# Branch B's scan: state products of two chunks in one visit, halves before full width, and the state update at once

## The chip, the core and the metric

One core of a Trainium2 chip runs one launch of a two-layer decoder trunk. The metric is the device time in microseconds (us) of that launch. TensorE (PE in the profile) does the matrix products, with weight loads shown apart as PEld; VectorE is DVE, ScalarE is ACT, GpSimd is POOL, and SP is the queue that issues nearly all DMA transfers.

## The reference, cut to what matters

Each layer normalises `x`, applies one wide input projection, and feeds four token mixers. Their outputs, each multiplied by a SiLU gate, are projected, merged by sigmoid gates, projected again and added to `x`. Mixer B is a gated DeltaNet with 4 heads and 256 tokens in 4 chunks of 64. Its scan over the chunks is what the change touches:

```python
def step(state, xs):
    q_i, k_i, u_i, w_i, qk_i, g_i = xs
    v_new = u_i - jnp.einsum('bhcd,bhde->bhce', w_i, state)
    o = (jnp.einsum('bhcd,bhde->bhce', q_i * jnp.exp(g_i)[..., None], state)
         + jnp.einsum('bhcm,bhme->bhce', qk_i, v_new))
    g_last = g_i[..., -1]
    state = (state * jnp.exp(g_last)[..., None, None]
             + jnp.einsum('bhcd,bhce->bhde', k_i * jnp.exp(g_last[..., None] - g_i)[..., None], v_new))
    return state, o
_, o = lax.scan(step, state0, xs)
```

The outputs `o` of all chunks are then RMS-normalised per head and go on to the gate.

## The kernel before, in words

All large weights are streamed from memory in pieces of 512 KB (`wr`, four buffers), cast on ACT to a high part (`wh`, L484) and split on DVE to a low part (`wl`, L485). A projection then runs three TensorE products for each piece: L594 to L596 for 512 columns (tiles `m`, `d`, `br`), L631 to L633 for 256 (tiles `z`, `b`). These follow each other as a list of items. The mixers are Python generators ("streams") that are advanced a step between two items: each `yield` ends a step, and what a step issues stands in program order there. The build then schedules the instructions of each engine by its own timeline, so a step's instructions come out interleaved with those of the items around it. On the chip each engine runs its list strictly in the order that results.

`branch_b` is such a stream. Its scan loops over `c` in 0..3. Two heads share a tile of 128 partitions (64 tokens each), so with `p` in 0, 1 a chunk is two such pairs. For each chunk:

- `pv` (L1075, L1078), the new values: for each `p` one product of full width (`U`, `vb`, out 128 partitions x 128 columns), then, where `c > 0`, two halves (`wT` with the state `st`), each of which writes 64 partitions. DVE copies `pv` to `vn` (L1081). Then the transposes `pot` of the chunk before (`out_T`, L1064).
- `po` (L1088, L1091), the outputs, after a `yield`: again, for each `p`, one product of full width (`Q`, `vn`), then two halves (`qgT`, `st`). ACT squares it (`sqo`), DVE sums (`ro`), DVE and POOL make the reciprocal root (`rsbo`, `ro`), DVE scales `po` to `on` (L1099).
- `pS` (L1107), the state's update, after another `yield`: four products with 64 rows each, two into each of two PSUM banks, and DVE adds them to the decayed state (`S`, L1114; L1111 for the first chunk).

So a chunk takes three visits. All of `pv`, `po`, `pS` and `pot` use the pool of two PSUM banks called "b"; tiles in SBUF come from a pool of 20 slabs "b", which the reloaded residual `xr` and the norm's weights `lng`, `lnb` share.

Three shapes of TensorE product matter: full (128 rows, 128 output partitions), halves (128 rows, 64 output partitions; the profile prints 128*64) and products of 64 rows (64*128; `pS`, and the scores `dsc` of mixer D). `dpo` of mixer D is also made of halves, and `dpt` of transposes of full width. An fp32 product of this size is two matmul records in the profile, a transpose one.

Of the kernel before, what the change touches and what calls it, by code (L numbers as in the profile page):

```python
# [15 lines left out]
ALU = mybir.AluOpType  # L16
# [4 lines left out]
P = 128  # L21
# [180 lines left out]
def kernel(ctx: ExitStack, tc: tile.TileContext, d, out, dbg=None, nlayers=DEPTH):  # L202
    nc = tc.nc
    V, A, T, G = nc.vector, nc.scalar, nc.tensor, nc.gpsimd
# [16 lines left out]
    def slab(which, shape, name):  # L221
        free = int(np.prod(shape[1:]))
        assert free <= 512, (name, shape)
        t = slabs[which].tile([P, 512], F32, tag="slab", name=name)[:shape[0], 0:free]
        if len(shape) == 3:
            t = t.rearrange("p (a b) -> p a b", b=shape[2])
        elif len(shape) == 4:
            t = t.rearrange("p (a b c) -> p a b c", b=shape[2], c=shape[3])
        return t

    def bank(which, shape, name):
        return banks[which].tile(shape, F32, tag=which, name=name)

    def fl(a):
        return a.rearrange("p a b -> p (a b)")
# [14 lines left out]
    def smc(name, i=0, n=1):  # L250
        lo = SM[name][0]
        return sm[:, lo + i:lo + i + n]
# [19 lines left out]
    def rstd(dst, src, bias, n, tag, mark=None):  # L272
        bt = tiny.tile([P, n], F32, tag=f"rsb{tag}", name=f"rsb{tag}")
        a = V.tensor_scalar(bt, src, bias, None, ALU.add)
        b = G.tensor_tensor(dst, bt, negh[:, 0:n], ALU.pow)
        if mark:
            marks[f"eps{mark}"], marks[f"pow{mark}"] = a, b
# [426 lines left out]
    def layer_items(l, prev):  # L704
# [161 lines left out]
        def branch_b():  # L866

            psel = bank("b", [P, 4, 2, 2, 2], f"psel{l}")
            for c in range(4):
                T.matmul(psel[:, c].rearrange("p k q h -> p (k q h)"), cfc("sel", c % 2), L.ckv[:, c // 2, 160:168],  # L870
                         start=True, stop=True)
            bd = sp.tile([P, 2, 4, 2], F32, tag="bd", name=f"bd{l}")
            for h2 in range(2):
                r = slice(64 * h2, 64 * h2 + 64)
# [28 lines left out]
            egl = sp.tile([P, 2, 8], F32, tag="b_egl", name=f"egl{l}")  # L903
# [9 lines left out]
            grp = []  # L913
            for g in range(2):
# [33 lines left out]
                vb = sb4("vb")  # L948
# [6 lines left out]
                kbg, ktil, qg = sb4("kbg"), sb4("ktil"), sb4("qg")  # L955
# [7 lines left out]
                qgT, dec = sb4("qgT"), sb4("dec")  # L963
                feat4([qgT], qg, "qg")
                pd = bank("b", [P, 4, P], f"pd{g}_{l}")
                for j in range(4):
                    T.matmul(pd[:, j, :], gcol[:, 4 * g + j:4 * g + j + 1].to_broadcast([P, P]), cfc("tri"),
                             start=True, stop=False)
# [4 lines left out]
                N, Q = sb4("N"), sb4("Q")  # L973
# [21 lines left out]
            for g in range(2):  # L995
                for j in range(4):
                    r = slice(32 * g + 8 * j, 32 * g + 8 * j + 8)
# [13 lines left out]
            for w in range(2):  # L1011
                for g in range(2):
                    for j in range(4):
                        r = slice(32 * g + 8 * j, 32 * g + 8 * j + 8)
                        nc.sync.dma_start(blocks(scr[1 + w, g], j), tb[r, w])
            yield
            inv = []
            for g in range(2):
                Ti, U = (slab("b", [P, 4, P], f"g_{nm}{g}_{l}") for nm in ("T", "U"))
                nc.sync.dma_start(fl(Ti), scr[1, g])  # L1020
                nc.sync.dma_start(fl(U), scr[2, g])
                inv.append((LLs[g], U, Ti))
            yield
            yield
            mk = lambda i: cu[:, i, :].unsqueeze(1).to_broadcast([P, 4, P])
            for li in range(2):
                Xs = []
                for g, (LL, U, Ti) in enumerate(inv):
                    px = bank("b", [P, 4, P], f"px{li}{g}_{l}")
                    for j in range(4):  # L1030
                        T.matmul(px[:, j, :], LL[:, j, :], U[:, j, :], start=True, stop=True)
                    Xs.append(slab("b", [P, 4, P], f"X{li}{g}_{l}"))
                    A.copy(Xs[g], px)
                yield
                for g, (LL, U, Ti) in enumerate(inv):
                    py = bank("b", [P, 4, P], f"py{li}{g}_{l}")
# [11 lines left out]
            wT = []  # L1048
# [10 lines left out]
            st = on = None  # L1059

            def out_T(c, on):
                pt = bank("b", [P, 2, 2, 64], f"pot{c}_{l}")
                for p in range(2):
                    T.transpose(pt[:, p].rearrange("p h i -> p (h i)"), on[:, p, :], ident)  # L1064
                for p in range(2):
                    A.activation(L.oT[1][p][:, :, 64 * c:64 * c + 64], pt[:, p], AF.Copy, scale=smc("onorm", l))

            for c in range(4):
                g = c // 2
                vb, ktil, qgT, _, Q, _ = grp[g]  # L1070
                U = inv[g][1]
                pv = bank("b", [P, 2, P], f"pv{c}_{l}")
                for p in range(2):
                    j = 2 * (c % 2) + p
                    T.matmul(pv[:, p, :], U[:, j, :], vb[:, j, :], start=True, stop=(c == 0))  # L1075
                    if c > 0:
                        for h2 in range(2):
                            T.matmul(pv[64 * h2:64 * h2 + 64, p, :], wT[g][:, j, 64 * h2:64 * h2 + 64],  # L1078
                                     st[:, 2 * p + h2, :], start=False, stop=True)
                vn = slab("b", [P, 2, P], f"vn{c}_{l}")  # L1080
                V.tensor_copy(vn, pv)  # L1081
                if on is not None:
                    out_T(c - 1, on)
                yield
                po = bank("b", [P, 2, P], f"po{c}_{l}")
                for p in range(2):
                    j = 2 * (c % 2) + p
                    T.matmul(po[:, p, :], Q[:, j, :], vn[:, p, :], start=True, stop=(c == 0))  # L1088
                    if c > 0:
                        for h2 in range(2):  # L1090
                            T.matmul(po[64 * h2:64 * h2 + 64, p, :], qgT[:, j, 64 * h2:64 * h2 + 64],  # L1091
                                     st[:, 2 * p + h2, :], start=False, stop=True)
                sq = slab("b", [P, 2, P], f"sqo{c}_{l}")
                A.activation(sq, po, AF.Square, scale=128.0 ** -0.5)
                ro = tiny.tile([P, 2], F32, tag="ro", name=f"ro{c}_{l}")
                V.tensor_reduce(ro, sq, AX.X, ALU.add)
                rstd(ro, ro, EPS, 2, "o")
                on = slab("b", [P, 2, P], f"on{c}_{l}")
                V.tensor_tensor(on, po, ro.unsqueeze(2).to_broadcast([P, 2, P]), ALU.mult)  # L1099
                if c < 3:  # L1100
                    yield
                    pS = [bank("b", [P, 2, P], f"pS{c}{h2}_{l}") for h2 in range(2)]
                    for p in range(2):
                        j = 2 * (c % 2) + p
                        for h2 in range(2):
                            r = slice(64 * h2, 64 * h2 + 64)
                            T.matmul(pS[h2][:, p, :], ktil[r, j, :], vn[r, p, :], start=True, stop=True)  # L1107
                    sn = slab("b", [P, 4, P], f"S{c}_{l}")
                    if c == 0:
                        for h2 in range(2):  # L1110
                            V.tensor_copy(sn.rearrange("p (q h) e -> p h q e", h=2)[:, h2], pS[h2])  # L1111
                    else:
                        for h in range(4):
                            V.scalar_tensor_tensor(sn[:, h, :], st[:, h, :],  # L1114
                                                   egl[:, h % 2, 2 * c + h // 2:2 * c + h // 2 + 1],
                                                   pS[h % 2][:, h // 2, :], ALU.mult, ALU.add)
                    st = sn
                yield
            out_T(3, on)


# [442 lines left out]
```

## Time and profile before

| what | value |
|---|---|
| median of 3 runs | 1056.73 us (1055.52 to 1058.17) |
| the profiled execution | 1053.03 us |
| its span, first to last instruction | 1050.9 us |
| PE busy | 1026.6 us, 98% |
| DVE, ACT, POOL busy | 718.8, 542.3, 27.3 us |
| mean granted TensorE clock | 0.993 of full speed |
| the scan in layer 0 | 288 to 374 us |
| the scan in layer 1 | 798 to 880 us |

The span is that of one profiled execution. Matmuls are pipelined and their ends are modelled, so what TensorE's work costs is read from the starts of its records: the time from one start to the next.

### The profile page before, as it was taken

What the parts mean: (1) busy time and instruction counts of PE and PEld (TensorE: products, weight loads), DVE (VectorE), ACT (ScalarE), POOL (GpSimd) and SP (SyncE); (2) the same over time, 40 slices, a digit from 0 to 9 for tenths busy, and PEclk for the clock granted to TensorE, in tenths of its full rate; (3) what the DMA queues carried; (4) which work ended last, traced back from release to release, by engine and by line L of the source; (5) the groups of instructions that cost most, each with busy time, mean ns of one, the idle gap of its engine ahead of it and who ended that gap; (6) DMA issues with size and microseconds to landing.
All of it is one profiled execution on the core that took longest, in us unless ns stands there. A gap on an engine that the chain in (4) does not pass through costs nothing.

```text
span 1050.9 us, 16072 instructions
## 1 busy us (share of the span) xinstructions
PE 1026.6 (98%) x5918; PEld 849.6 (81%) x5918; DVE 718.8 (68%) x1579; ACT 542.3 (52%) x1012; POOL 27.3 (3%) x37
## 2 busy tenths in 40 slices
PE   6999999999999999999999999999999999999996
PEld 6589897888887788888866998888789778888885
DVE  3788768886666656766684887798837555566676
ACT  2276675654453445555426567566545444555550
POOL 0000000000000000000000000000100000000000
PEclk9999999999999999999999999999999999999998
DMA  9973335557654476545824444456563337544551
GB/s 335 329 250 121 121 124 168 202 175 236 228 162 165 138 276 224 159 143 179 303 74 163 139 123 123 149 201 199 174 236 128 102 119 227 172 163 141 169 172 41
DMA packets 67406, 185.18 MB, mean 176 GB/s; under 512 B 13696, under 2 KB 17152, under 8 KB 67328
## 3 DMA queue, kind: packets, MB, share of 16 engines
q1 hardware_dynamic: 67328, 184.16, 52.7%
q8 instruction: 47, 0.77, 0.3%
q14 instruction: 31, 0.25, 0.1%
HBM read 179.67 MB, written 4.46 MB: 175 GB/s over the span
## 4 chain that ended last, share of the span: by engine, by line
PE 88%; DVE 4%; DMA 4%; ACT 1%; issue 1%; SPq 1%; DVEq 0%; ACTq 0%
PE m L594 6%; PE m L595 5%; PE m L596 5%; PE first L602 5%; PE d L594 4%; PE d L595 4%; PE d L596 4%; PE z L631 3%; PE z L632 3%; PE z L633 3%; PE br L594 3%; PE br L596 3%; PE br L595 3%; PE b L631 2%; PE b L632 2%; PE b L633 2%
## 5 line engine op out<-in xcount | busy, mean ns | idle before, releaser
L485 DVE TENSOR_TENSOR wl<-wr,wh 128x1024 fp32r<-128x1024 f32 x248 | 302.4, 1223 | 171.4 <-ACT wh L484 168.6
L484 ACT CAST wh<-wr 128x1024 fp32r<-128x1024 f32 x248 | 259.9, 1050 | 216.7 <-issue 41.9
L594 PE MATMUL m<-wh,hh 128*128 128x512 f32 x256 | 102.8, 401 | 0.4 <-DVE ml L1421 0.3
L594 PE MATMUL d<-wh,hh 128*128 128x512 f32 x256 | 103.0, 402 | 0.0
L595 PE MATMUL m<-wl,hh 128*128 128x512 f32 x256 | 101.9, 398 | 0.0
L595 PE MATMUL d<-wl,hh 128*128 128x512 f32 x256 | 101.2, 395 | 0.0
L596 PE MATMUL d<-wh,hl 128*128 128x512 f32 x256 | 101.1, 395 | 0.0
L596 PE MATMUL m<-wh,hl 128*128 128x512 f32 x256 | 100.6, 393 | 0.0
L631 PE MATMUL z<-hh,wh 128*128 128x256 f32 x256 | 74.1, 289 | 0.0
L632 PE MATMUL z<-hl,wh 128*128 128x256 f32 x256 | 73.4, 287 | 0.0
L633 PE MATMUL z<-hh,wl 128*128 128x256 f32 x256 | 73.3, 286 | 0.0
L305 DVE SCALAR_TENSOR_TENSOR ada<-wada,cact,ada 128x512 f32<-128x512 f32 x77 | 57.5, 747 | 18.7 <-DMA wada<-in_wada 17.9
L631 PE MATMUL b<-hh,wh 128*128 128x256 f32 x192 | 57.6, 300 | 2.8 <-ACT ckv L832 2.3
L594 PEld LDWEIGHTS m<-wh,hh 128*128 128x128 f32 x256 | 48.1, 188 | 11.8 <-issue 1.0
L596 PEld LDWEIGHTS d<-wh,hl 128*128 128x128 f32 x256 | 48.5, 189 | 10.4 <-issue 0.4
L595 PEld LDWEIGHTS d<-wl,hh 128*128 128x128 f32 x256 | 48.5, 190 | 9.8 <-DVE wl L485 0.3
L594 PEld LDWEIGHTS d<-wh,hh 128*128 128x128 f32 x256 | 48.5, 189 | 9.8 <-issue 0.6
L596 PEld LDWEIGHTS m<-wh,hl 128*128 128x128 f32 x256 | 48.1, 188 | 10.0 <-issue 0.3
L595 PEld LDWEIGHTS m<-wl,hh 128*128 128x128 f32 x256 | 48.1, 188 | 9.9 <-issue 1.0
L633 PE MATMUL b<-hh,wl 128*128 128x256 f32 x192 | 55.4, 288 | 0.0
L632 PE MATMUL b<-hl,wh 128*128 128x256 f32 x192 | 55.3, 288 | 0.0
L594 PE MATMUL br<-wh,bh 128*128 128x512 f32 x128 | 51.7, 407 | 0.0
(355 smaller groups left out, 2123.7 us busy)
## 6 DMA issues: line engine op xcount, KB each, us to landing
wr<-in_win SPq DMA_DIRECT2D x208, 512.0 KB
wr<-in_wbr SPq DMA_DIRECT2D x32, 512.0 KB
wada<-in_wada SPq DMA_DIRECT2D x32, 512.0 KB
wada<-in_wada SPq DMA_DIRECT2D x32, 256.0 KB
wro<-in_wout SPq DMA_DIRECT2D x8, 512.0 KB
wr<-in_wout SPq DMA_DIRECT2D x8, 512.0 KB
wrs<-in_win SPq DMA_DIRECT2D x8, 256.0 KB
wrearly<-in_win SPq DMA_DIRECT2D x8, 256.0 KB
```

The source lines that it names most:

```text
L305: return V.scalar_tensor_tensor(acc, w, cd, acc, ALU.mult, ALU.add)
L484: marks["hi"] = A.copy(hi, src)
L485: return [V.tensor_tensor(lo, src, hi.bitcast(F32), ALU.subtract)]
L594: ins.append(T.matmul(ps, a, wh, start=(first and i == 0), stop=False))
L595: ins.append(T.matmul(ps, a, wl, start=False, stop=False))
L596: ins.append(T.matmul(ps, b, wh, start=False, stop=(last and i == 1)))
L602: return [T.matmul(ps, a(2 * p + i, t), w[p](i * n, n), start=(first and i == 0), stop=(last and i == 1)) for i in range(2)]
L631: T.matmul(ps[:, f, :], wh, hh(k), start=(k == 0), stop=False)
L632: T.matmul(ps[:, f, :], wh, hl(k), start=False, stop=False)
L633: T.matmul(ps[:, f, :], wl, hh(k), start=False, stop=(k == nk - 1))
```

## The change

The scan is written with helpers: `from_state` issues the four halves of a chunk, `within` the two products of full width. The visit of chunk `c` now issues first the halves of `pv` for `c`, then (from `c = 2` on) the halves of `po` for `c - 1` with the state before (`before`), then the full products of `pv` for `c` and of `po` for `c - 1`. The accumulation's start flag moves with it, to the first product issued in a bank. The state's update `pS` follows in the next step, without the step that `po` had between. `out_T` is issued a step later than `normed`. The last chunk's outputs form a visit of their own. There are 8 steps where there were 11. No product, copy or transfer is added or taken away.

```diff
-            for c in range(4):
-                g = c // 2
-                vb, ktil, qgT, _, Q, _ = grp[g]
-                U = inv[g][1]
-                pv = bank("b", [P, 2, P], f"pv{c}_{l}")
+            def from_state(dst, lhs, c, st):
+
                 for p in range(2):
                     j = 2 * (c % 2) + p
-                    T.matmul(pv[:, p, :], U[:, j, :], vb[:, j, :], start=True, stop=(c == 0))
-                    if c > 0:
-                        for h2 in range(2):
-                            T.matmul(pv[64 * h2:64 * h2 + 64, p, :], wT[g][:, j, 64 * h2:64 * h2 + 64],
-                                     st[:, 2 * p + h2, :], start=False, stop=True)
...
+                    for h2 in range(2):
+                        T.matmul(dst[64 * h2:64 * h2 + 64, p, :], lhs[:, j, 64 * h2:64 * h2 + 64],
+                                 st[:, 2 * p + h2, :], start=(p == 0), stop=False, skip_group_check=True)
+
+            def within(dst, lhs, rhs, c):
                 for p in range(2):
                     j = 2 * (c % 2) + p
...
+                    T.matmul(dst[:, p, :], lhs[:, j, :], rhs(p, j), start=(c == 0 and p == 0), stop=True,
+                             skip_group_check=True)
...
+            before = None
+            for c in range(4):
+                g = c // 2
+                egc = lambda h: egl[:, h % 2, 2 * c + h // 2:2 * c + h // 2 + 1]
+                pv = bank("b", [P, 2, P], f"pv{c}_{l}")
+                if c > 0:
+                    po = bank("b", [P, 2, P], f"po{c - 1}_{l}")
+                    from_state(pv, wT[g], c, st)
+                    if c > 1:
+                        from_state(po, grp[(c - 1) // 2][2], c - 1, before)
+                values(pv, c)
+                if c > 0:
+                    outputs(po, c - 1, vn)
+                vn = slab("b", [P, 2, P], f"vn{c}_{l}")
+                V.tensor_copy(vn, pv)
+                if c > 0:
+                    on = normed(c - 1, po)
+                yield
                 if c < 3:
-                    yield
                     pS = [bank("b", [P, 2, P], f"pS{c}{h2}_{l}") for h2 in range(2)]
...
-                    st = sn
-                yield
+                    before, st = st, sn
+                    yield
+                    if c > 0:
+                        out_T(c - 1, on)
+                else:
+                    po = bank("b", [P, 2, P], f"po3_{l}")
+                    from_state(po, grp[1][2], 3, st)
+                    outputs(po, 3, vn)
+                    out_T(2, on)
+                    on = normed(3, po)
+            yield
             out_T(3, on)
```

TensorE in layer 1, the outputs of chunk 2 among the products `m` of a gate projection; before, they stand alone and change between full width (128x128) and halves (64x128):

```order
L596 MATMUL m_10_8750<-wh_2_8473,hl_5567 128x512
L1088 MATMUL po_1_8776<-vn_1_8687,g_Q_1_7448 128x128
L1091 MATMUL po_1_8776<-S_1_8646,g_qgT_1_7331 64x128 x2
L1088 MATMUL po_1_8776<-vn_1_8687,g_Q_1_7448 128x128
L1091 MATMUL po_1_8776<-S_1_8646,g_qgT_1_7331 64x128 x2
L594 MATMUL m_11_8763<-wh_1_8467,hh_5566 128x512
```

The same outputs of chunk 2 after the change:

```order
L595 MATMUL m_10_8786<-wl_1_8477,hh_5566 128x512
L1073 MATMUL pv_1_8705<-S_1_8666,wT_1_8184 64x128 x4
L1073 MATMUL po_1_8706<-S_1_8524,g_qgT_1_7331 64x128 x4
L1079 MATMUL pv_1_8705<-g_vb_1_7210,g_U_1_7775 128x128 x2
L1079 MATMUL po_1_8706<-vn_1_8590,g_Q_1_7448 128x128 x2
L1384 MATMUL dpo_1_8730<-PT_1_8676,dvv_1_8045 64x128
```

They share a visit with the new values of chunk 3: eight halves in a row, then four products of full width.

TensorE in layer 0, the new values of chunk 1, before; the schedule has parted the two halves of one pair and put products `m` between them:

```order
L1075 MATMUL pv_0_3411<-g_vb_0_1618,g_U_0_2636 128x128
L1078 MATMUL pv_0_3411<-S_0_3322,wT_0_3066 64x128
L594 MATMUL m_01_3398<-wh_1_3144,hh_143 128x512
L595 MATMUL m_01_3398<-wl_1_3145,hh_143 128x512
L596 MATMUL m_01_3398<-wh_1_3144,hl_144 128x512
L594 MATMUL m_01_3398<-wh_1_3144,hh_143 128x512
L1078 MATMUL pv_0_3411<-S_0_3322,wT_0_3066 64x128
L1075 MATMUL pv_0_3411<-g_vb_0_1618,g_U_0_2636 128x128
L1078 MATMUL pv_0_3411<-S_0_3322,wT_0_3066 64x128 x2
L1064 MATMUL pot_0_3420<-cf,on_0_3227 128x128 x2
```

The new values of chunk 1 after the change:

```order
L633 MATMUL z_0_3256<-hh_143,wl_1_3030 128x256
L1073 MATMUL pv_0_3313<-S_0_3223,wT_0_3066 64x128 x4
L1079 MATMUL pv_0_3313<-g_vb_0_1618,g_U_0_2636 128x128 x2
L1079 MATMUL po_0_3314<-vn_0_3111,g_Q_0_1905 128x128 x2
L1384 MATMUL dpo_0_3338<-PT_0_3235,dvv_0_2923 64x128
```

The four halves stand together, earlier in the program (among `z`), and the outputs of chunk 0 follow in the same visit.

TensorE in layer 0 after the change, the state's update of chunk 1, whose second half (`pS_0_3421`) takes the bank that the outputs of chunk 0 (`po_0_3314` above) held:

```order
L596 MATMUL m_00_3394<-wh_2_3150,hl_144 128x512
L1122 MATMUL pS_0_3420<-vn_0_3323,g_ktil_0_1674 128x128 x2
L594 MATMUL m_01_3407<-wh_1_3144,hh_143 128x512
L595 MATMUL m_01_3407<-wl_1_3145,hh_143 128x512
L596 MATMUL m_01_3407<-wh_1_3144,hl_144 128x512
L1122 MATMUL pS_0_3421<-vn_0_3323,g_ktil_0_1674 128x128 x2
L1376 MATMUL dpt_0_3441<-cf,prd_0_3356 128x128 x4
```

Between `po_0_3314` and `pS_0_3421` stand 14 products of mixer D, 27 of `m` and the first half of `pS`.

## Rows read from the trace of the kernel before

**Rows 1.** The page's first two parts: TensorE's busy time, granted clock in 40 slices

```profile
PE 1026.6 (98%) x5918; PEld 849.6 (81%) x5918; DVE 718.8 (68%) x1579; ACT 542.3 (52%) x1012; POOL 27.3 (3%) x37
...
PEclk9999999999999999999999999999999999999998
```

**Rows 2.** Waits of TensorE, whole span: total us, times, longest

```profile
PE adac L338 <- DVE bnsta L764: 8.2, 1, 8.2
...
PE pu L1045 <- DVE g_U L1039: 1.0, 1, 1.0
...
PE adac L316 <- DVE ada L305: 0.2, 1, 0.2
```

**Rows 3.** Busy time by stretch: us, then PE, PEld, DVE, ACT, POOL, clock, DMA

```profile
300.00:325.00 25.00, 25.00 (x144) 18.73 (x140) 17.62 (x33) 10.40 (x18) 0.70 (x1) 1.00 0.51 168
```

**Rows 4.** TensorE's timeline, layer 1, outputs of chunk 2: start, us, records

```profile
847.56 0.40 PE L596 MATMUL m<-wh,hl 128*128 128x512 f32 x1
847.79 0.39 PE L1088 MATMUL po<-vn,g_Q 128*128 128x128 f32 x2
848.11 0.44 PE L1091 MATMUL po<-S,g_qgT 128*64 128x128 f32 x4
848.48 0.49 PE L1088 MATMUL po<-vn,g_Q 128*128 128x128 f32 x2
848.90 0.44 PE L1091 MATMUL po<-S,g_qgT 128*64 128x128 f32 x4
849.26 0.50 PE L594 MATMUL m<-wh,hh 128*128 128x512 f32 x1
849.60 0.39 PE L595 MATMUL m<-wl,hh 128*128 128x512 f32 x1
```

**Rows 5.** TensorE's timeline, layer 0, outputs of chunk 0, full width alone

```profile
292.35 0.28 PE L632 MATMUL z<-hl,wh 128*128 128x256 f32 x1
292.47 0.61 PE L1088 MATMUL po<-vn,g_Q 128*128 128x128 f32 x4
...
293.04 0.28 PE L631 MATMUL z<-hh,wh 128*128 128x256 f32 x1
```

**Rows 6.** TensorE's timeline, layer 0, a run of eight halves of mixer D

```profile
364.03 1.09 PE L1361 MATMUL dpo<-PT,dvv 128*64 128x128 f32 x16
365.06 0.49 PE L1088 MATMUL po<-vn,g_Q 128*128 128x128 f32 x2
```

**Rows 7.** TensorE's timeline, layer 0, new values of chunk 1, a half alone

```profile
307.44 0.38 PE L1075 MATMUL pv<-g_vb,g_U 128*128 128x128 f32 x2
307.75 0.43 PE L1078 MATMUL pv<-S,wT 128*64 128x128 f32 x2
308.12 0.50 PE L594 MATMUL m<-wh,hh 128*128 128x512 f32 x1
```

**Rows 8.** TensorE's timeline, state's update: half of one, then a whole one

```profile
301.91 0.71 PE L1107 MATMUL pS<-vn,g_ktil 64*128 64x128 f32 x4
302.55 0.50 PE L594 MATMUL m<-wh,hh 128*128 128x512 f32 x1
...
855.42 0.72 PE L1107 MATMUL pS<-vn,g_ktil 64*128 64x128 f32 x8
856.08 0.65 PE L1353 MATMUL dpt<-cf,prd 128*128 128x128 f32 x4
```

**Rows 9.** Tile `po`: count, ns min/median/max, first and last start in us

```profile
L1088 PE MATMUL po<-vn,g_Q x32: 270/275/377, 292.5 to 869.5; 128*128 128x128 f32 x32
...
L1099 DVE TENSOR_TENSOR on<-po,ro x8: 417/419/425, 301.4 to 872.8; 128x256 f32<-128x256 f32 x8
```

**Rows 10.** Waits of the SP queue: total us, times, longest

```profile
SPq L548 <- DVE wl L485: 477.6, 156, 11.8
```

**Rows 11.** Chain that ended last, in order of time: one weight transfer

```profile
250.74 7.24 DMA wr<-in_win
```

**Rows 12.** The page's costliest groups: busy us, mean ns of one

```profile
L485 DVE TENSOR_TENSOR wl<-wr,wh 128x1024 fp32r<-128x1024 f32 x248 | 302.4, 1223 | 171.4 <-ACT wh L484 168.6
```

More of the change, by code (lines that the diff above doesn't have):

```diff
@@ L1066, in out_T, with values, outputs, normed @@
                     A.activation(L.oT[1][p][:, :, 64 * c:64 * c + 64], pt[:, p], AF.Copy, scale=smc("onorm", l))
-            for c in range(4):
-                g = c // 2
-                vb, ktil, qgT, _, Q, _ = grp[g]
-                U = inv[g][1]
-                pv = bank("b", [P, 2, P], f"pv{c}_{l}")
+            def from_state(dst, lhs, c, st):
                 for p in range(2):
                     j = 2 * (c % 2) + p
-                    T.matmul(pv[:, p, :], U[:, j, :], vb[:, j, :], start=True, stop=(c == 0))
-                    if c > 0:
-                        for h2 in range(2):
-                            T.matmul(pv[64 * h2:64 * h2 + 64, p, :], wT[g][:, j, 64 * h2:64 * h2 + 64],
-                                     st[:, 2 * p + h2, :], start=False, stop=True)
[L1080 to L1083, printed above, removed]
-                yield
-                po = bank("b", [P, 2, P], f"po{c}_{l}")
+                    for h2 in range(2):
+                        T.matmul(dst[64 * h2:64 * h2 + 64, p, :], lhs[:, j, 64 * h2:64 * h2 + 64],
+                                 st[:, 2 * p + h2, :], start=(p == 0), stop=False, skip_group_check=True)
+            def within(dst, lhs, rhs, c):
                 for p in range(2):
                     j = 2 * (c % 2) + p
[L1088 to L1092, printed above, removed]
+                    T.matmul(dst[:, p, :], lhs[:, j, :], rhs(p, j), start=(c == 0 and p == 0), stop=True,
+                             skip_group_check=True)
+            def values(pv, c):
+                within(pv, inv[c // 2][1], lambda p, j: grp[c // 2][0][:, j, :], c)
+            def outputs(po, c, vn):
+                within(po, grp[c // 2][4], lambda p, j: vn[:, p, :], c)
+            def normed(c, po):
                 sq = slab("b", [P, 2, P], f"sqo{c}_{l}")
@@ L1099, in branch_b @@
                 V.tensor_tensor(on, po, ro.unsqueeze(2).to_broadcast([P, 2, P]), ALU.mult)
+                return on
+            before = None
[16 more added lines that the diff above has]
+                yield
                 if c < 3:
-                    yield
                     pS = [bank("b", [P, 2, P], f"pS{c}{h2}_{l}") for h2 in range(2)]
@@ L1106, in branch_b @@
                             r = slice(64 * h2, 64 * h2 + 64)
-                            T.matmul(pS[h2][:, p, :], ktil[r, j, :], vn[r, p, :], start=True, stop=True)
+                            T.matmul(pS[h2][:, p, :], grp[g][1][r, j, :], vn[r, p, :], start=True, stop=True)
                     sn = slab("b", [P, 4, P], f"S{c}_{l}")
@@ L1113, in branch_b @@
                         for h in range(4):
-                            V.scalar_tensor_tensor(sn[:, h, :], st[:, h, :],
-                                                   egl[:, h % 2, 2 * c + h // 2:2 * c + h // 2 + 1],
-                                                   pS[h % 2][:, h // 2, :], ALU.mult, ALU.add)
-                    st = sn
-                yield
+                            V.scalar_tensor_tensor(sn[:, h, :], st[:, h, :], egc(h), pS[h % 2][:, h // 2, :],
+                                                   ALU.mult, ALU.add)
+                    before, st = st, sn
[9 more added lines that the diff above has]
+            yield
             out_T(3, on)
```

## The prediction

> **What bounds the kernel now.** I read the page first. TensorE is busy in 98% of the span and no other engine comes above 68%; its granted clock is full in every slice of the 40 [rows 1]. Busy time alone doesn't show a bound, since a matmul that waits for its place in the pipeline counts as busy, so I went on to what TensorE waits for. There is one long wait at the start (8.2 us); after the first 60 us the longest is 1.0 us, and the list ends at 0.2 us [rows 2]. In a stretch in the middle of the scan TensorE is busy for 25.00 of 25.00 us, with DVE at 17.62 and ACT at 10.40 [rows 3]. The weights don't pace it either: the SP queue waits 156 times, 477.6 us in all, for DVE to free a `wr` buffer [rows 10], so transfers wait for the consumer and not the consumer for transfers. From some 60 us on, then, the time is the sum of TensorE's steps from start to start, and a microsecond taken from these in the scan should come off the end.
>
> Next I read what a step costs where the shape of the product changes. Full-width products alone: the outputs of chunk 0 start at 292.47 and the second `z` after them at 293.04; less one `z` step (292.35 to 292.47, 0.12) that is 0.45 for two products, 0.22 each [rows 5]. Halves in a run: eight of them, four pairs, take 1.03 from their start to the next start, while one pair alone takes 0.37 (848.11 to 848.48) [rows 4, 6]; three more pairs cost 0.66, so 0.22 a pair. With changes of shape: from the `m` ahead of the outputs of chunk 2 to the second `m` behind them lie 2.04 us [rows 4]. Two `m` steps are 0.46 (847.56 to 847.79 is 0.23), two full products 0.45, two pairs 0.44. That leaves 0.69 us for four changes (full to halves, back, again, and back to `m`), 0.17 each. The page tells where it goes: the full product between two pairs holds 0.42 and not 0.22, a pair 0.37 and not 0.22, and the first `m` after a pair 0.34 and not 0.23 [rows 4].
>
> **The change, part by part.** It takes no product away, so everything it gives is in the order.
>
> *Changes of shape.* I counted them in the order of TensorE's instructions over the whole program, each place where a product of one of the three shapes (full, halves, 64 rows) follows one of another: 185 before, 149 after. Between full and halves there are 93 and then 61, between full and 64 rows 77 and 79, between halves and 64 rows 15 and 9. For the price, the least is 0.10 (the first full product to the first pair, 0.32 for 0.22, [rows 4]). The most comes from putting the new block together: 0.10 to enter, eight halves 1.03 [rows 6], a full product after halves 0.27 (0.42 less the 0.15 for leaving to halves again), three more at 0.22, in all 2.06, against 3.16 for two visits like that of chunk 2 (2 x 1.58): 1.10 for six changes, 0.18 each. Changes to 64 rows look cheaper: an update of four such products, two pairs, holds 0.66 for 0.44 [rows 8], 0.11 for each of its two. I take 0.15 over all kinds: 36 x 0.15 = 5.4 us, between 3.6 and 6.5.
>
> [...]
>
> *Halves that stand alone.* In five visits the schedule had parted a pair. One half alone holds 0.37 (307.75 to 308.12, [rows 7]), as long as a pair does, so a parted pair costs a pair more, 0.22 beside its changes. After the change I count one such visit. 4 x 0.22 = 0.9 us. The bounds are 0 (if the single ones overlap with what follows) and 4 x 0.37 = 1.5.
>
> *The state's update.* Where its two banks don't come free together, its products are issued in two parts of two. Such a part takes 0.64 us (301.91 to 302.55), and a whole update of four 0.66 (855.42 to 856.08) [rows 8]: the part saves nothing. Five of six updates were split, now four. One split less is 0.64, of which two changes (0.30) are counted above: 0.3 us, between 0 and 0.64.
>
> *New waits.* `pv` and `po` now hold both banks of pool "b" in one visit, and the second part of `pS` waits until `on` has been read out of the bank of `po`. Behind it in TensorE's queue stands everything. From `po` to the end of `on` it took 9.3 us the first time (292.5 to 301.4, and 0.42) and 3.7 the last (869.5 to 872.8) [rows 9]. In layer 0, 27 `m` (6.2 us at 0.23), a run of eight `dpo` (1.03) and a part of `pS` (0.64) stand between `po` and that part, 7.9 us beside six score products, so it may or may not be late by a microsecond once. Nothing in the trace has this wait as it will be. Bounds: 0, as in the scan now, and 2.0, twice the longest wait of [rows 2] after the start. I take 0.6, nearer to the lower end, since every present visit of the scan meets its inputs in time.
>
> *Moved for nothing.* DVE and ACT issue the same instructions in another order, hidden under TensorE (7.4 and 14.6 us free in 25, [rows 3]). On SP, in layer 1, the loads of `xr`, `lng` and `lnb` (eight of them) move ahead of some weight pieces. The pieces behind them are issued at least 85 products before their first use, as before (87); at 0.23 that is over 19 us, against 7.2 for a slow transfer [rows 11] and 1.2 for the split [rows 12]. If that cover were gone, the price would be one transfer, 7 us.
>
> **The sum.** 5.4 + 0.9 + 0.3 - 0.6 = 6.0 us less. The profiled execution took 1053.03 (span 1050.9), which gives 1047.0 (1044.9). That execution lies 3.7 us below the median of the runs, so I set the same difference against the median: 1056.73 - 6.0 = **1050.7 us**, 0.57% less. Its own range is 1048.1 to 1052.5: the lowest price with the middle of the rest (3.6 + 0.6 = 4.2 us less), and the highest of all with no wait (6.5 + 1.5 + 0.6 = 8.6). A measurement of this kernel can tell about 0.3%, 3.2 us, from no change.
>
> **The rivals.**
>
> 1. [...] Chance 0.2. [...]
>
> 2. *The banks: slower.* Every visit from chunk 1 on waits for `on` before the second part of `pS` or the next `po`. There are four such parts and two visits of the last chunk in the two layers. If `on` comes 9.3 us after `po` each time, as in the first [rows 9], and 7.9 us or less of other work stands between, TensorE stops for 1.5 us or more at each, 9 us at all six, and with a stop of the same kind at the next `pv`, for which the state comes as much later, 12: 1056.7 - 6.6 + 12 = 1062. It turns from gain to loss at a mean of 1.1 us a place, and is told as slower from 1.6 on. Against it: the last time it took 3.7. Chance 0.08. [...]
>
> 3. *More than the sum.* All changes at 0.18, halves and split at their upper bounds and no wait give 8.6, and some more if the steps freed let pairs with `dpo` overlap, up to 10: 1047. Chance 0.1.
>
> **How the numbers follow.** The forecast has 0.62, the rivals 0.2, 0.08 and 0.1. Faster by over 0.3%: the forecast but for its thin end near 3.2 (0.6), and rival 3 (0.1), and a little of rival 1 (0.02): 0.72. Within: 0.2. Slower: 0.08. The range leaves out most of rival 2 and the outer ends of 1 and 3: 1046.0 to 1057.0.
>
> **What would show it.** Right: in the profile after, a visit of eight halves and four full products that takes about 2.1 us beside two `m` steps, TensorE's stretches of the scan still busy throughout, the scan's stretch shorter by some 3 to 4 us in layer 0 (where 26 or so of the 36 changes go) and 2 in layer 1, and everything after it only shifted. Wrong: `pS` or `pv` in TensorE's list of waits, released by DVE's `on` or `S`, with a microsecond or more each (rival 2); or the full products after halves dearer than 0.42 (rival 1); or weight pieces late around the loads of `xr` in layer 1.

## The result and the profile after

The changed kernel takes 1045.73 us (median of 9 runs, 1042.98 to 1050.46) against 1054.41 for the kernel before (9 runs, 1051.83 to 1058.17, the three of the forecast's baseline among them): a ratio of 0.9918, 95% interval 0.9899 to 0.9937. Measured once more with 5 runs against 17 of before it was 1045.76 against 1053.53, ratio 0.9923 (0.9911 to 0.9935). So it is about 8 us faster. The forecast of 1050.7 was 5.0 us too high, and the time fell 0.27 us below the stated range, which began at 1046.0.

The profiled execution of after (1050.46, span 1048.7) is the slowest of its nine runs, so the profile of the second measurement (1045.80, span 1044.0) is used beside it. First TensorE's list of waits in the first one, whole span, which answers to [rows 2]; columns are total us, times, longest:

```profile
PE adac L338 <- DVE bnsta L764: 8.5, 1, 8.5
PE b L631 <- ACT ckv L832: 3.7, 1, 3.7
PE pu L1045 <- DVE g_U L1039: 2.2, 1, 2.2
PE hT L728 <- ACT xn L481: 1.4, 1, 1.4
PE tu_d L649 <- DVE tkd L451: 1.1, 2, 1.0
PE b L631 <- ACT qkva L655: 0.8, 1, 0.8
PE d L595 <- DVE wl L485: 0.5, 1, 0.5
PE m L594 <- DVE ml L1444: 0.4, 1, 0.4
PE adac L316 <- DVE ada L305: 0.2, 1, 0.2
```

No line names `pv`, `po` or `pS`: the waits that the prediction feared did not come. Two lines are new, `tu_d` and `d` behind `tkd` and `wl`. The wait of 1.0 us of `tu_d` and that of `d` stand near 400 us, after the scan of layer 0; the other one of `tu_d` (0.2) stands at 242 us. The `pu` wait stands ahead of the scan: it was 1.0 us before, is 2.2 here and 0.5 in the second profile of the same kernel, so it belongs to the execution.

Busy time by stretch, the two scans with what surrounds them, which answers to [rows 3] (us, then PE, PEld, DVE, ACT, POOL, granted clock, DMA share, GB/s):

```profile
285.00:385.00 100.00, 100.00 (x641) 83.55 (x641) 66.89 (x127) 47.31 (x81) 2.96 (x4) 1.00 0.53 174
780.00:870.00 90.00, 90.00 (x598) 74.44 (x597) 52.56 (x95) 44.02 (x75) 2.79 (x4) 1.00 0.44 144
```

TensorE is busy throughout, at full granted clock, so the gain is in the length of its steps. A visit of new values and outputs together, layer 1, which answers to [rows 4] (start us, us, records; a product is two records):

```profile
842.75 0.39 PE L595 MATMUL m<-wl,hh 128*128 128x512 f32 x1
843.06 0.66 PE L1073 MATMUL pv<-S,wT 128*64 128x128 f32 x8
843.55 0.61 PE L1073 MATMUL po<-S,g_qgT 128*64 128x128 f32 x8
844.09 0.71 PE L1079 MATMUL pv<-g_vb,g_U 128*128 128x128 f32 x4
844.64 0.61 PE L1079 MATMUL po<-vn,g_Q 128*128 128x128 f32 x4
845.18 1.09 PE L1384 MATMUL dpo<-PT,dvv 128*64 128x128 f32 x16
```

Eight halves and four full products lie between 843.06 and 845.18, 2.12 us; the prediction put the block together as 2.06. The change from halves to full (843.55 to 844.09, 0.54 for two pairs, and 1.03 for all eight halves, as for those of [rows 6]) costs what the old ones did, and there is one of it where there were several.

To see where the time went, the start of the same TensorE instruction is compared in two traces, before and after; the difference is a shift, and the change of the shift over a stretch is what the stretch gained (negative is shorter). Each number below is the difference of the medians of the shifts within 2 us of the stretch's ends (285, 385, 412, 780 and 880 us of the trace of before). Changes of shape are counted in the order of the instructions, by layer, less those of before.

| kernel | changes, layer 0 / 1 | scan of layer 0 | 385 to 412 | scan of layer 1 |
|---|---|---|---|---|
| changed | -26 / -10 | -6.21 | +2.07 | -1.54 |
| changed, again | -26 / -10 | -6.20 | +0.99 | -1.55 |
| mixed visits | -10 / +1 | -3.30 | -0.05 | +0.04 |
| halves first alone | -16 / -12 | -3.64 | -0.30 | -1.84 |
| update at once | -11 / -5 | -2.51 | +1.29 | -1.64 |
| update at once, halves first | -21 / -14 | -4.37 | +1.79 | -3.04 |
| outputs copied first | -28 / -11 | -6.34 | +2.00 | -2.07 |

The two profiles of the changed kernel agree on each scan to 0.01 us: -7.75 together. Then part of it is paid back at once, 2.07 in one and 0.99 in the other, which leaves 5.7 and 6.8 us, where the medians show 8.7 and 7.8. Where the rest lies is not shown: between 412 and 780 us the second profile gained a further 1.2 and the first lost 0.6. The other rows are the experiments below.

### The profile page after: what moved, and what is told of

Same layout as the page of the kernel before. It is cut to its first block, busy times and chain, and to the rows that moved or that the text cites. A ratio compares the mean times of both kernels' runs of the same rounds, so it can differ in the third digit from the quotient of the medians.

```text
span 1048.7 us, 16078 instructions
## 1 busy us (share of the span) xinstructions
PE 1019.4 (97%) x5918; PEld 847.4 (81%) x5918; DVE 718.4 (69%) x1579; ACT 541.9 (52%) x1012; POOL 26.8 (3%) x37
## 4 chain that ended last, share of the span: by engine, by line
PE 83%; DMA 10%; DVE 4%; ACT 1%; issue 1%; SPq 1%; DVEq 0%; ACTq 0%
PE m L594 6%; PE m L595 5%; PE m L596 5%; DMA wada<-in_wada 4%; PE d L595 4%; PE d L596 4%; PE d L594 4%; DMA wr<-in_win 3%; PE z L631 3%; PE z L633 3%; PE z L632 3%; PE br L594 3%; PE br L596 3%; PE br L595 3%; PE b L631 2%; PE b L632 2%
```

## The experiments

Theory: the time of the scan is products plus a fixed price for each change of shape, and no wait. First rival: the gaps at a change hide work that is paid elsewhere, so fewer changes bring little. Second: it is the sharing of visits, or the earlier state, that brings the gain, and not the count.

**The price by itself.** Each layer of the changed kernel gets a block of 16 full products and 16 pairs of halves into a bank of its own that nobody reads, once in turns, once grouped. The block is work added to the kernel.

```
+            for i in range(16):
+                dm_full()
+            for i in range(16):        # in turns: this line is left out
+                dm_pair()
```

In turns: 

> The changed kernel with a block of extra products ahead of the scan in each layer, 16 of full width and 16 pairs of halves, alternating one full product and one pair; nobody reads what they write. Only the difference to the grouped block counts: 60 changes of shape more over both layers. Price theory: 60 x 0.15 = 9 us slower than the grouped block (7 to 11). Rival (0.05 or less a change): 3 us or less.

Grouped: 

> The changed kernel with the same extra products, 16 of full width first and then 16 pairs. By the steps of 0.22 us each the 32 extra steps in each layer take 7.0 us, 14 us over both layers, and the two or three changes of a block under 1 us: about 14 to 15 us slower than the changed kernel. If work on TensorE is not what bounds the scan's stretch, less.

Measured: 1073.93 us in turns (ratio 1.0203, 1.0182 to 1.0225) and 1062.95 grouped (1.0088, 1.0072 to 1.0104), on one chip. 11.0 us for 60 changes more is 0.18 each. The timeline of the block in turns, layer 0:

```profile
289.26 1.06 PE L1052 MATMUL pw<-g_U,g_kbg 128*128 128x128 f32 x8
290.16 0.39 PE L1101 MATMUL dm<-g_vb,g_U 128*128 128x128 f32 x2
290.47 0.44 PE L1106 MATMUL dm<-g_vb,wT 128*64 128x128 f32 x4
290.84 0.49 PE L1101 MATMUL dm<-g_vb,g_U 128*128 128x128 f32 x2
291.26 0.44 PE L1106 MATMUL dm<-g_vb,wT 128*64 128x128 f32 x4
...
302.29 0.44 PE L1106 MATMUL dm<-g_vb,wT 128*64 128x128 f32 x4
302.65 0.71 PE L1079 MATMUL pv<-g_vb,g_U 128*128 128x128 f32 x4
```

And grouped:

```profile
290.88 3.74 PE L1101 MATMUL dm<-g_vb,g_U 128*128 128x128 f32 x32
294.55 3.71 PE L1106 MATMUL dm<-g_vb,wT 128*64 128x128 f32 x64
298.19 0.71 PE L1079 MATMUL pv<-g_vb,g_U 128*128 128x128 f32 x4
```

The block lasts 12.49 us (290.16 to 302.65) or 7.31 (290.88 to 298.19); layer 1 shows 12.50 and 7.31. So 30 changes cost 5.18, 0.173 each: 0.42 instead of 0.23 for a full product ahead of a pair, 0.37 instead of 0.23 for a pair. This is the cleanest price of the study, and the first rival falls with it: at 0.05 a change, the most that its expectation allows, the 30 would make 1.5 us, where the trace has 5.18. It is the price of a change between full products and halves; the blocks hold no product of 64 rows. What a change spends its 0.173 us on is shown by no run here.

A miss: the grouped kernel lies 17 to 18 us above the changed one, where 14 to 15 were expected. The two blocks account for 14.6. In the table's terms, layer 0's scan less its block gained 4.88 instead of 6.2, 1.3 us less, and layer 1's as much as ever. Where the rest of some 2 us is, is not shown.

**One part of the change at a time.** Shared visits and the early update kept, but full products and halves in turns as before (the edit in short):

```
-    from_state(pv, wT[g], c, st); from_state(po, ..., before)
-    values(pv, c); outputs(po, c - 1, vn)
+    mixed(pv, ..., c, st)                # one full, one pair, one full, one pair
+    mixed(po, ..., c - 1, before)
```

> The visits stay merged and the state's update stays in the next step, but within a visit full products and halves alternate again as before the change. In TensorE's order there are 176 changes of shape (149 in the changed kernel, 185 before); lone halves and split updates are as in the changed kernel. Price theory (0.15 us a change): 27 x 0.15 = 4.1 us slower than the changed kernel, so about 4.6 us faster than before (ratio about 0.9956). Rival 'the visits give the gain' (merging, fewer steps; a change costs 0.05 or less): at most 1.4 us slower than the changed kernel, 7.3 us or more faster than before (ratio about 0.993).

Measured: 1049.82 us, ratio 0.9963 (0.9948 to 0.9977), the value of the theory. The changed kernel has 27 changes fewer and is some 4.7 us faster by the two ratios (0.9918 and 0.9963 of 1053.65), 0.17 to 0.18 each; by the scans in the table it is 7.75 against 3.26, 0.166 each.

The kernel before with its visits and steps as they were, halves ahead of full products in each (in short):

```
-    T.matmul(pv[:, p, :], ...full...); two halves         # for each p
+    two halves for each p, then the full product for each p
```

> The kernel before, with the halves ahead of the full products in each visit, and nothing else: steps, visits and the update's place are those of before. 157 changes of shape (185 before). Price theory: 28 x 0.15 = 4.2 us faster than before, and some of the lone halves (up to 0.9 us) as well, ratio about 0.995 to 0.996. Rival 'the visits give the gain': 1.4 us or less faster than before, ratio 0.9985 or more.

Measured: 1048.64 us, 0.995 (0.9935 to 0.9965): 5.0 us for 28 changes, at the upper end of the theory. This alone is more than half of the gain, without a shared visit.

The kernel before with the state's update one step after the values, and the outputs in a step of their own behind it; then the same with halves first:

```
     V.tensor_copy(vn, pv)
     yield
+    pS ..., sn ...                       # was behind po
+    yield
     po = bank(...)                       # still with the old state
```

Update at once: 

> The kernel before with only the third part of the change: the state update stands one step after the values, and the outputs, with the old state, in a step of their own behind it; full products and halves alternate as before. Counted in the order of the instructions: 169 changes of shape (185 before), lone halves 1 visit (5), split state updates 1 (5). Price theory: 16 x 0.175 = 2.8, lone halves 0.9, splits 4 x 0.3 = 1.2, together 4.9 us less than before, ratio 0.9953, with no wait of TensorE in the scan. First rival (only changes of shape count): 2.8 us, ratio 0.9973. Second rival (an update that follows the values at once waits for their copy, some 0.5 us in each of 6 visits, and eats the rest): ratio 0.998 to 1.0, with waits of pS on vn in the profile.

With halves first: 

> As the update at once alone, and in each visit all halves ahead of all full products; values and outputs stay in visits of their own, so nothing is shared. 150 changes of shape (149 in the changed kernel), split updates 1 (4 in the changed kernel). Price theory: 35 x 0.175 = 6.1, lone halves 0.9, splits 1.2, together 8.2 us less than before, ratio 0.9922, within 1 us of the changed kernel. Rival (the shared visit is worth something beyond the count of changes): 2 us or more slower than the changed kernel, ratio 0.995 or above.

Measured: 1049.71 us, 0.9968 (0.9953 to 0.9984), and 1047.36, 0.9944 (0.9929 to 0.9958). The theory's numbers (0.9953, 0.9922) lie at the edge of the first interval and outside the second; both times lie by what the changes of shape alone make, 2.8 us (the first one's rival) and, with 35 x 0.175, 6.1. The second is 1.6 us above the changed kernel measured beside it, between the 1 of its theory and the 2 of its rival. TensorE has no wait on `vn` or `S` in either scan, so the second rival of the first falls. The scans themselves gained 4.15 and 7.41 (table), of which 1.29 and 1.79 were paid back after the scan of layer 0. So two things were wrong in the expectations: they had no pay-back, and they had 1.2 us for four split updates. With 0.173 a change, the scans leave 1.4 us for halves and splits in both kernels, and 0.9 of it was set down to lone halves. If that holds, the split updates brought at most half of what was expected.

The changed kernel once more: 

> The changed kernel once more, with more rounds. Price theory (0.17 to 0.18 us for each of the 36 changes of shape that are gone, as the alternating and the grouped block showed, 0.9 for lone halves, 0.3 for the split update, no new waits): 7.3 to 7.7 us less than before, ratio 0.993. Rival (the prediction's own sum with 0.15 a change and 0.6 of new waits; what went beyond it in the first comparison was the spread of a baseline of few runs): 6.0 us, ratio 0.9943 or above. In the profile: if the two waits of TensorE near 397 us (some 2 us together, on weights that came late) were caused by the shorter scan, they stand there again; if they belong to that one execution, they are under 0.7 us there.

Measured: 0.9923, 7.8 us, the theory's end. Of the two waits at 400 us one stands there again (`tu_d`, 1.0 us), the other does not. That lies between the expectation's two cases, some 2 us and under 0.7.

Outputs copied by ScalarE first, so that their bank is free sooner:

```
+    on = slab(...); A.copy(on, po)
-    A.activation(sq, po, AF.Square, ...)
+    A.activation(sq, on, AF.Square, ...)
-    V.tensor_tensor(on, po, ro...)
+    V.tensor_tensor(on, on, ro...)
```

> The changed kernel, with one copy more in each of the 8 norms of the outputs: ScalarE copies the bank po to its slab first, and square and scale read the slab, so the bank is given back one copy after its last product and not after square, sum, root and scale. Counted: 146 changes of shape (149). Price theory: 39 x 0.175 = 6.8, lone halves 0.9, splits 0.3 to 0.9, together 8 to 8.6 us less than before, ratio 0.992, that is 0.5 to 1 us below the changed kernel of the same call. Rival (the copies, 8 x about 0.4 us on ScalarE, stand ahead of conversions of weights that TensorE waits for, or lengthen the path to the outputs' transposes): 1 us or more above the changed kernel.

Measured: 1044.29 us, 0.9912 (0.9898 to 0.9927), 1.5 us under the changed kernel measured beside it, a little more than expected; the intervals overlap, so it is not shown to be better.

**What pays back at 400 us.** In the first profile of after, ScalarE, then VectorE and TensorE near that place:

```profile
399.80 1.05 ACT L484 CAST wh<-wr 128x1024 fp32r<-128x1024 f32 x1 [3.59 <-DMA wr<-in_win]
```

```profile
400.19 0.28 DVE L450 TENSOR_TENSOR tkd<-d,cc 128x128 f32<-128x128 f32 x1
400.88 1.23 DVE L485 TENSOR_TENSOR wl<-wr,wh 128x1024 fp32r<-128x1024 f32 x1 [0.41 <-ACT wh L484]
402.02 0.28 DVE L451 TENSOR_TENSOR tkd<-tkd,ropet_d 128x128 f32<-128x128 f32 x1
402.45 0.63 PE L649 MATMUL tu_d<-cf,tkd 128*128 128x128 f32 x4 [0.96 <-DVE tkd L451]
```

The same piece and product before:

```profile
401.44 1.05 ACT L484 CAST wh<-wr 128x1024 fp32r<-128x1024 f32 x1 [2.39 <-DMA wr<-in_win]
404.10 0.63 PE L649 MATMUL tu_d<-cf,tkd 128*128 128x128 f32 x4
```

A weight piece lands at 399.8; `wh` and `wl` are made of it; and the last 0.28 us of `tkd`, a rotation that is half done, stands behind this `wl` in VectorE's queue. TensorE wants `tkd` for `tu_d`. In the kernel before, the order on VectorE is the same, the piece landed at 401.44, and `tu_d` started at 404.10 without a wait; in after it could have started some 2 us sooner than its 402.45. The piece came 1.6 us sooner, TensorE 3.7, and the difference is what was paid back. It is so in each profile of the table: 5.34 less 4.35 in the second profile (0.99 paid back), 2.14 less 0.87 with the update at once (1.29), 6.34 less 4.56 with halves first too (1.79), 7.50 less 5.51 with the outputs copied (2.00). Where the piece came as much sooner as TensorE or more, nothing was: mixed visits (1.91 against 1.85) and halves first alone (5.40 against 4.03). Ahead of these pieces in the SP queue stand the four loads of `xr` and the four of `lng` and `lnb`, which are used some 150 us later. Four kernels put them behind the weights of the last branch, by one dependence of order:

```
     def load_out(_):
+        L.late = marks["load"]           # the last weight load so far
+        L.xr = load_x(L.xsrc, f"xr{l}", L.late)
...
-    nc.sync.dma_start(lnw[i][b], ...)
+    in_order(L.late, nc.sync.dma_start(lnw[i][b], ...))
```

The norm's rows alone: 

> The changed kernel, with the loads of the last norm's rows (lng, lnb: four of 256 KB, used only some 150 us later) issued behind the weights of the last branch and not between the rows x and the weight pieces of d at 380 us. Theory (part of what the scan of layer 0 gains is paid back near 400 us, because the weight pieces of d come behind these loads): the weights land some 2 to 3 us sooner, TensorE gives back under 0.7 us between 385 and 412 us in place of 1.0 to 2.1, and the time is 0.5 to 1 us under the changed kernel's, ratio 0.9915. Rival (the pieces are late because their buffers come free late, or because the transfer engines are full whatever stands ahead): the same 1 to 2 us are given back, ratio 0.9923 as the changed kernel.

Both: 

> As the one with the norm's rows later, and the four loads of the rows x (256 KB each) behind them too, so that nothing but weights stands in the queue near 380 us. Theory: the give-back near 400 us is gone (under 0.3 us), 1 to 1.5 us under the changed kernel's time, ratio 0.991. Rival: no change, 0.9923; or the loads collide where they now stand, near 475 us, with the last branch's weights: 0.994 and a new wait of TensorE between 470 and 560 us.

Both, outputs copied first: 

> The version with the outputs copied first, and the rows x and the norm's rows loaded later. Theory: both gains add: 1 to 2 us under the copy alone, ratio 0.990. Rival: as the copy alone, 0.991.

The kernel before, both: 

> Control: the kernel before, with the rows x and the norm's rows loaded later. Its TensorE waits for nothing between 385 and 412 us, so by the theory (the shorter scan runs into these loads) there is nothing to win: ratio 0.9995 to 1.0005. Rival (the loads cost any version something): 0.9985 or below.

Measured, beside a before of 1054.07: 1056.21 (1.0016, 1.0 to 1.0033), 1044.02 (0.9902, 0.9877 to 0.9928), 1045.22 (0.9902, 0.9876 to 0.9928) and 1051.47 (0.9976, 0.9958 to 0.9995). The changed kernel did not run beside them, so only the ratios compare. At its place the theory came true with the norm's rows alone: the piece came 5.26 us sooner and TensorE 4.04, `tu_d` does not wait, and nothing is paid back (-0.28 from 385 to 412). The time did not follow (below). The piece and `tu_d` there:

```profile
396.19 1.05 ACT L484 CAST wh<-wr 128x1024 fp32r<-128x1024 f32 x1 [1.76 <-DMA wr<-in_win]
399.78 0.60 PE L649 MATMUL tu_d<-cf,tkd 128*128 128x128 f32 x4
```

With both moved the theory fell: the ratios (0.990) are about what it said, but the intervals hold the rivals' too, and the stretch 385 to 412 still pays back 1.18 and 1.06 us. The same chain is there:

```profile
395.50 1.05 ACT L486 CAST wh<-wr 128x1024 fp32r<-128x1024 f32 x1 [3.94 <-DMA wr<-in_win]
```

```profile
396.58 1.22 DVE L487 TENSOR_TENSOR wl<-wr,wh 128x1024 fp32r<-128x1024 f32 x1 [0.95 <-ACT wh L486]
397.72 0.28 DVE L453 TENSOR_TENSOR tkd<-tkd,ropet_d 128x128 f32<-128x128 f32 x1
```

ScalarE waits 3.94 us for the piece although nothing but weights is queued ahead. And the control, which pays nothing back, gained 2.6 us by the move where the theory gave it nothing, as its rival said; the changed kernel gained some 2 by the ratios. So what the move is worth is not the pay-back. The piece lands 5.1 us after its issue in after and 3.7 with both moved, but the issue itself waits for VectorE in either (394.67 and 391.78 us). What holds that issue up with both moved, and not with the norm's rows alone, stays open; a `wl` that doesn't part the two halves of `tkd` was not tried.

The kernel with only the norm's rows moved is 10 us slower than the changed one, which nobody expected. Its timeline near the end of layer 0, where `lng` and `lnb` now stand ahead of `wro`:

```profile
494.03 1.14 ACT L484 CAST who<-wro 128x512 fp32r<-128x512 f32 x2 [3.58 <-DMA wro<-in_wout]
...
502.20 1.04 ACT L484 CAST wh<-wr 128x1024 fp32r<-128x1024 f32 x1 [1.32 <-DMA wr<-in_wbr]
503.15 0.59 ACT L1411 ACTIVATE mg<-m 128x512 f32<-128x512 f32 x1
```

```profile
500.03 0.60 PE L1439 MATMUL mT<-cf,acc 128*128 128x128 f32 x4
503.80 0.80 PE L594 MATMUL m<-wh,hh 128*128 128x512 f32 x1 [3.17 <-ACT mg L1411]
504.39 0.63 PE L595 MATMUL m<-wl,hh 128*128 128x512 f32 x1
504.82 0.63 PE L596 MATMUL m<-wh,hl 128*128 128x512 f32 x1
```

ScalarE's `mg`, which frees a bank for TensorE, is queued behind casts that wait for `wro` and `wr`. TensorE stops for 3.2 us, and then each `m` takes 0.43 us instead of 0.23. There is a second such stop in layer 1 (3.7 us). In the two changed kernels with `xr` moved too, the first `wro` is issued ahead of `lng`, and neither stop is in their lists.

## Why the prediction was right, and where not

**The bound** held: TensorE's steps, busy for 100.00 of 100 and 90.00 of 90 us in the scans of after, and each microsecond taken from the scan shifted what follows, but for the pay-back. Two readings of it were off, and nothing hangs on them: the granted clock is below 0.9 in the last of the 40 slices, and the longest wait after the first 60 us is 1.4 us and not 1.0 (`hT`, at 540 us; its line in the list above is the same before).

**Changes of shape.** The count of 36 was right, the price too low. The step that failed is "I take 0.15 over all kinds"; the blocks measured 0.173 in the trace and 0.18 by the times, the upper end of the stated bounds, so the term is 6.2 to 6.5 us and not 5.4. What drew it down was the discount for changes to 64 rows, though by the prediction's own counts (93 to 61) 32 of the 36 lie between full and halves. Whether that discount holds for the others is not shown, since no block tests them. With 0.173 for each change, the scans of all seven profiles in the table leave 0.6 to 1.7 us in layer 0 and -0.24 to +0.78 in layer 1.

**Halves that stand alone and the state's update.** 0.9 and 0.3 were predicted. The scans leave 7.75 - 36 x 0.173 = 1.5 us for both, all of it in layer 0. The two were not told apart; that a split update is worth little rests only on the update at once, above. Of the count of parted pairs the prediction saw a part: five became one among `pv` and `po`, but in the trace after two pairs of `dpo` are parted that were whole before, so three are left, and at its 0.22 the term is 0.4 and not 0.9. One of them, in layer 1:

```profile
828.76 0.71 PE L1079 MATMUL po<-vn,g_Q 128*128 128x128 f32 x4
829.40 0.43 PE L1384 MATMUL dpo<-PT,dvv 128*64 128x128 f32 x2
829.76 0.50 PE L594 MATMUL br<-wh,bh 128*128 128x512 f32 x1
```

What makes up the rest of the 1.5 us stays open.

**New waits.** "I take 0.6" failed too: there were none in the scan, the lower end of the bounds. So the scans give 6.2 + 1.5 = 7.75 us less where the sum said 6.0.

**Moved for nothing, everything after only shifted.** Not quite. The cover was said to be gone at worst "around the loads of `xr` in layer 1"; it was layer 0, where 0.99 to 2.07 us are given back. By layers, 3 to 4 us were expected in layer 0 and 2 in layer 1; 6.2 (4.1 to 5.2 after the pay-back) and 1.5 came.

**The base.** The other failed step is "so I set the same difference against the median": 1056.73 was the median of three runs, and with more runs the median was 1054.41 (9, these three among them), and later 1053.65 (11), 1053.53 (17) and 1054.07 (23). The profiled execution (1053.03) was near the true level, and the 3.7 us added to it were spread of the three. Against 1053.03 the same sum gave 1047.0, inside the range. So of the 5.0 us of error, 2.3 are the base (1056.73 - 1054.41) and 2.7 the size of the gain (8.7 and not 6.0): 1.75 of these stand in the scans, less the pay-back, and the others are not placed. The range had no term for the base's own spread.

**The rivals.** Rival 1 (0.05 or less a change, a price that no run shows) is shown wrong by the blocks: 0.173. Rival 2 (banks) is shown wrong by the list of waits. Rival 3 (all at the upper bounds, no wait, 8.6) is what came closest, 8.7 and 7.8 by the two pairs of medians, though partly by luck: it had no pay-back, and the lone halves are not at their upper bound. The likeliest case had the right mechanism with too low a price. Halves first alone brings 5.0 us, the early update and the shared visits without it 3.8, and all of it 7.8 to 8.7.

**A better version.** Copying the outputs first, or loading `xr` and the norm's rows later, gives medians of 1044.0 to 1045.2, up to 1.7 us under the changed kernel, with intervals that overlap its own: not told apart from it.

## What to carry over

Where an engine is busy throughout, count what follows what: a fixed price at each change of shape, measured as a block in turns against the same block grouped, gave the gain of layer 1's scan within 0.8 us and 0.6 to 1.7 us too little for layer 0's, over kernels that reached their order in different ways. Set a forecast against several runs, or give the baseline's spread a term of its own: here it was as large as a third of the effect. And ask of each gain on the bounding engine where the next thing that doesn't move with it stands: here a weight piece that came 1.6 us sooner where TensorE came 3.7, with a 0.28 us instruction queued behind it.

## What the runs showed that was not expected

- This stop of TensorE cost more than its length. The kernel with the norm's rows moved, by stretch, layer 0 (columns as above):

```profile
495.00:500.00 5.00, 5.00 (x23) 4.08 (x22) 5.00 (x9) 4.01 (x9) 0.00 (x0) 1.00 0.52 145
500.00:504.00 4.00, 0.83 (x6) 0.56 (x5) 3.30 (x6) 2.68 (x6) 0.00 (x0) 0.84 0.93 298
504.00:510.00 6.00, 6.00 (x16) 4.67 (x17) 2.40 (x4) 1.98 (x4) 0.00 (x0) 0.54 0.64 229
510.00:516.00 6.00, 6.00 (x28) 4.95 (x27) 3.67 (x3) 3.01 (x4) 0.00 (x0) 1.00 0.80 265
```

  TensorE was idle for 3.17 of the 4 us from 500 on, the granted clock of the next 6 us is 0.54, against 1.00 in the 6 us after, and only 16 matmuls ran in them, where those after hold 28. Compared with the trace of before, the stop itself lost 2.9 us, and 13 `m` steps of 0.43 to 0.59 us in place of 0.23 some 2.7 more.
- The two profiles of the changed kernel agree on the gain of each scan to 0.01 us, while their spans differ by 4.7 us (1048.7 and 1044.0). By the shifts, 1.7 of it arise near 274 us (the `pu` wait), 1.1 near 400, 1.4 between 430 and 560 and 0.5 between 560 and 700: the spread lies outside the scans, at waits and transfers.
